# Layer 1's mixer in a two-layer fp32 trunk: a bank for the second spatial turn, spatial products at other steps, subtractions and square sums on VectorE

## The chip, the core and the metric

The kernel runs on one core of one Trainium2 chip, in one launch. The metric is the device time of an execution in microseconds: 994.84 as the median of 3 runs before the change. Of two kernels the faster is the one with the lower time; a difference counts from about 0.2%, 2 us.

TensorE multiplies, VectorE and ScalarE do elementwise work and can read PSUM, GpSimd does some elementwise work in SBUF and issues some DMAs, and SyncE's queue (SP) issues the loads of the weights.

## What is computed

An input x of 512 positions by 1024 features passes through two layers, each with a mixer and a gated feed-forward network (FFN) behind an RMS norm, and a final norm. Layer 1's mixer and the FFN are the parts that matter here:

```python
def chunked_spatial_gating(u, v, sgu_norm, w_spatial, b_spatial):
    b, s, _ = u.shape
    n = s // CHUNK                       # 4 chunks of 128 positions
    vn = rms_norm(v, sgu_norm).reshape(b, n, CHUNK, C_HEADS, C_HEAD_DIM)
    mask = jnp.tril(jnp.ones((CHUNK, CHUNK), dtype=w_spatial.dtype))
    ws = w_spatial * mask                # 8 heads, 128 x 128
    gate = jnp.einsum('hts,bnshc->bnthc', ws, vn) + b_spatial.T[None, None, :, :, None]
    return u * gate.reshape(b, s, C_WIDTH)

def gated_conv_ffn(x, w_gate, w_up, conv_w, conv_b, w_down):
    g = causal_dwconv3(jnp.einsum('bsd,df->bsf', x, w_gate), conv_w) + conv_b
    up = jnp.einsum('bsd,df->bsf', x, w_up)
    return jnp.einsum('bsf,fd->bsd', jax.nn.silu(g) * up, w_down)
```

In layer 1, u and v are the two halves of gelu(norm(h) @ w_in_odd), 1024 features each; the gated product goes through w_out_odd and is added to h.

## The kernel before

**Numbers.** Everything is float32. A factor is held as a high part, rounded to the type that TensorE multiplies fast (fp32r), and a low part, the remainder; a product is three matmuls, high by high, high by low and low by high (`mm3`, lines 132 to 135). A loaded block of weights (tag "raw", 4 buffers, issued on SP's queue) is split in one of two ways into tiles of 6 buffers each. `parts` (L127 to L129): ScalarE copies the high part, VectorE subtracts it for the low part. `summed` (L118 to L122): ScalarE writes the negated block as `lo` (L120), a DMA issued on GpSimd's queue adds the block to it (L121), ScalarE copies the high part (L122). A raw buffer is given to the next load when its readers are done, the accumulating DMA among them.

**PSUM.** Seven banks of 128x512 rotate among all products (`mm_bank`, L45); an eighth (`aux_bank`, L48) is shared by transposes and small sums. The instructions of one engine run in the order that a scheduler has fixed at build time; only semaphores order the engines against each other. A bank is given on when its last reader is done.

**Layer by layer.** h is kept feature by position, 8 tiles of 128x512. A projection loops over k, the 8 feature tiles, for four output banks. Each time a tile of h is complete, `Norm.add` writes its high and low part for the next stage (`hgh` on ScalarE, L175; `hgl` on VectorE, L176) and `Norm.square` adds its square to a running sum: the first square is written to the sum, the middle ones are squared on ScalarE (L188) and added on GpSimd (L189), the last is kept apart in some norms. The sums of squares over features are made with TensorE (`sst`, L197) and turned into 1/rms, which is applied after the projection.

**Layer 1's mixer** (`mixer1`) runs so: `u0`, the first half of u, over k; v, as a seven-product scheme with sums of blocks (`v_blocks`, L876; products in the order 1, 2, 6, 5, 7, 3, 4); `u1`, the second half of u, over k with four banks held throughout; then the output projection `oo` in two halves. The v scheme takes eight weight blocks as they are or summed; for products 7 and 4 it splits them with `summed`, for the others with `parts`. Between the products 2 and 6, `turn_spatial` (L1001) transposes the eight 128x128 spatial matrices in two groups of four (the tiles `wst`), each group into one bank, from which ScalarE takes the high and VectorE the low part (L1011, L1012). Both groups use the aux bank.

When v is complete, its norm's factor `rc_v` is worked out (square root on ScalarE, reciprocal and corrections on VectorE), and v is split into `vnh` (L1055) and `vnl` (L1056), eight tiles each, four per half of the heads. A spatial product (`spatial(j)`, one per head) is one `mm3` into a rotating bank `sp`, which VectorE multiplies by a gain into `gt` (L1072). `gated(j)` adds the bias and multiplies by u (L1079). `turned(j)` transposes `gt` into another bank `mT` (L1091) and splits it into `mx` (L1093, L1094), the moving factor of `oo`. These steps are set between the k-steps of `u1` and `oo` by a callback ahead of each k.

**The FFN.** Its gate and up projections use a seven-product scheme too (`both`, with sums of weight blocks `s12`, `s34` for gate and up; ScalarE and VectorE split them, L648 and L649); parts of products are kept (`kept`, L697, L707) while others run. The first pair of feature blocks of each layer is multiplied directly, before the norm's factor is applied to h; there the evacuation (`direct.evacuate`) multiplies by 1/rms: the gate's rows on VectorE (L571), then the convolution (L509), silu (ScalarE, L520), a multiply of the result by 1/rms on GpSimd (L574, two per layer), and the multiply of up by the result on VectorE (L577). The results are split again for the down projection (in layer 1 by `part`, L1149 to L1151).

Of the kernel before, what the change touches and what calls it, by code (L numbers as in the profile page):

```python
# [30 lines left out]
def tile_trunk(ctx: ExitStack, tc: tile.TileContext, x, norm_mix, norm_ffn, final_norm,  # L31
# [134 lines left out]
    class Norm:  # L166
# [13 lines left out]
        def square(self, k, order=lambda ins: ins):  # L180
            if self.n == 0:
                order(nc.scalar.activation(self.ssq, h[k], AF.Square))
            elif self.n == NK - 1 and self.apart:
                self.last = tp.tile([P, S], F32, tag="rstd", name=f"last_{self.name}")
                order(nc.scalar.activation(self.last, h[k], AF.Square))
            else:
                sq = tp.tile([P, S], F32, tag="sq", name=f"sq_{self.name}{k}")
                order(nc.scalar.activation(sq, h[k], AF.Square))  # L188
                nc.gpsimd.tensor_tensor(self.ssq, self.ssq, sq, ALU.add)  # L189
            self.n += 1  # L190

        def rstd_tokens(self):
# [296 lines left out]
    class Ffn:  # L489
# [58 lines left out]
        def direct(self, f, normed, sets, ch, before=lambda i, j: None):  # L548

            layer = self.layer  # L550
            banks = {}
            for js in sets:
                for i, k in enumerate(PAIRS):
                    for j in js:
                        before(i, j)
                        hi, lo = ch["gu"[j // 2], i // 4]
                        c = slice((j % 2) * P, (j % 2 + 1) * P)
                        if j not in banks:
                            banks[j] = mm_bank(f"gu{layer}_{f}_{j}")
                        mm3(banks[j], (hi[:, i % 4, c], lo[:, i % 4, c]), hg_k(k),  # L560
                            i == 0, i == NK - 1)

            def evacuate():
                r = self.r
                gates = []
                for j in range(2):
                    t = padded_tile()
                    if normed:
                        nc.scalar.copy(t[:, 2:], banks[j])
                    else:  # L570
                        nc.vector.tensor_tensor(t[:, 2:], banks[j], r, ALU.mult)  # L571
                    s = self.silu(self.conv(t, f + j), f + j)
                    if not normed:
                        nc.gpsimd.tensor_tensor(s, s, r, ALU.mult)  # L574
                    gates.append(s)
                for j, s in enumerate(gates):
                    nc.vector.tensor_tensor(s, banks[2 + j], s, ALU.mult)  # L577
                    self.act(f + j, s)

            return evacuate  # L580
# [65 lines left out]

        def halves(self, hi, lo, src):
            nc.scalar.activation(hi, src, AF.Copy)  # L648
            nc.vector.tensor_tensor(lo, src, hi.bitcast(F32), ALU.subtract)  # L649

        def both(self, f):

            layer, ap, n = self.layer, self.ap, f"{self.layer}_{f}"
            raws = ffn_weights(layer, f, [(key, half) for half in range(2) for key in "gu"])
            stat = {}

            def put(key, product, hi_lo, i):
                stat[key, product] = hi_lo[0][:, i], hi_lo[1][:, i]

            w = self.unit(f"a11_{n}")  # L660
            for i, key in enumerate("gu"):
                self.halves(w[0][:, i], w[1][:, i], raws[key, 0][0][:, :, :P])
                put(key, 1, w, i)
            for key in "gu":
                r0, r1 = raws[key, 0][0], raws[key, 1][0]
                s12, s34 = (wp.tile([P, 2, 4, P], F32, tag="sum", bufs=3, name=f"{x}{key}_{n}")
                            for x in ("s12", "s34"))
                nc.vector.tensor_tensor(s12[:, 0], r0[:, :, P:], r1[:, :, P:], ALU.add)
                nc.vector.tensor_tensor(s12[:, 1], s12[:, 0], r0[:, :, :P], ALU.subtract)  # L669
                w = self.unit(f"s12{key}_{n}")  # L670
                self.halves(*w, s12)
                put(key, 5, w, 0)
                put(key, 6, w, 1)
                nc.vector.tensor_tensor(s34[:, 0], r0[:, :, :P], r0[:, :, P:], ALU.subtract)
                nc.vector.tensor_tensor(s34[:, 1], r1[:, :, :P], s12[:, 1], ALU.subtract)
                hi, lo = (parts if f == NF - 2 else summed)(*raws[key, 1])
                for i, product in enumerate((2, 4)):
                    c = slice(i * P, (i + 1) * P)
                    stat[key, product] = hi[:, :, c], lo[:, :, c]
                w = self.unit(f"s34{key}_{n}")  # L680
                self.halves(*w, s34)
                put(key, 7, w, 0)
                put(key, 3, w, 1)

            banks = {"g": {}, "u": {}}
            kept = ap.tile([P, 3, HALF], F32, tag="kept", bufs=1, name=f"kept{n}")
            pads = [padded_tile() for _ in range(2)]
            lo, hi = slice(2, 2 + HALF), slice(2 + HALF, 2 + S)
            dst = {("g", 1): pads[0][:, lo], ("g", 6): pads[0][:, hi], ("g", 7): pads[1][:, hi],
                   ("g", 4): pads[1][:, lo]}  # L690
            dst.update({("u", product): kept[:, i, :] for i, product in enumerate((1, 6, 7))})
            onto = {2: 1, 5: 7, 3: 6}
            s, pending = {}, {}

            def after(key, product, ps):
                if (key, product) in dst:
                    nc.scalar.copy(dst[key, product], ps)  # L697
                elif product == 5 and (key, 7) not in pending:
                    pending[key, 5] = ps
                elif product in onto:  # L700
                    d = dst[key, onto[product]]
                    nc.vector.tensor_tensor(d, ps, d, ALU.add)  # L702
                if (key, product) == ("u", 4):
                    pending["u", 4] = ps
                if product == 7:
                    d = dst[key, 7]
                    nc.vector.tensor_tensor(d, pending[key, 5], d, ALU.add)  # L707

            for key, product in (("g", 1), ("u", 1), ("g", 5), ("g", 6), ("u", 5), ("u", 6),
                                 ("g", 2), ("g", 7), ("u", 2), ("u", 7), ("g", 4), ("g", 3),  # L710
                                 ("u", 4), ("u", 3)):
                after(key, product, self.multiply(banks[key], f"{key}{n}", product,
                                                  stat[key, product]))
                if (key, product) == ("g", 4):
                    s[1] = self.silu(self.conv(pads[1], f + 1), f + 1)
                elif (key, product) == ("g", 3):
                    s[0] = self.silu(self.conv(pads[0], f), f)
            nc.vector.tensor_tensor(s[1][:, HALF:], kept[:, 2, :], s[1][:, HALF:], ALU.mult)
            nc.vector.tensor_tensor(s[1][:, :HALF], pending["u", 4], s[1][:, :HALF], ALU.mult)
            self.act(f + 1, s[1])  # L720
            s0 = s[0].rearrange("p (a b) -> p a b", a=2)
            nc.vector.tensor_tensor(s0, kept[:, :2, :], s0, ALU.mult)
            self.act(f, s[0])
# [152 lines left out]
    def v_blocks(mp, w, v, v_gelu, loads, turn_spatial):  # L876
# [100 lines left out]
        turn_spatial()  # L977
        multiply(6, "a", keep(0, 1))
        for i in range(2):
            give(7, i, b12[i], True)  # L980
        multiply(5, "e", lambda i, ps: None)
        multiply(7, "a", c22)
        for i in range(2):
            give(3, i, last[i])
            give(4, i, b21[i], True)
        multiply(3, "e", c12)
        multiply(4, "a", lambda i, ps: v_gelu(2 + i, 0, ps))

    def mixer1(norm):
        w = w_in_odd[0]  # L990
        with tc.tile_pool(name="m1", bufs=1) as mp:
# [9 lines left out]
            def turn_spatial():  # L1001
# [1 line left out]
                wsT.append(wp.tile([P, NK, P], F32R, tag="sum", bufs=3, name="wsT_lo"))  # L1003
                wsT_hi, wsT_lo = wsT
                for q in range(2):
                    ps = aux_bank(f"wst{q}")
                    for i in range(4):
                        nc.tensor.transpose(ps[:, i * P : (i + 1) * P], ws[:, 4 * q + i, :], ident)
                    hi = wsT_hi[:, 4 * q : 4 * q + 4, :]
# [74 lines left out]
            def turned(j):  # L1084
# [9 lines left out]
                nc.vector.tensor_tensor(lo, ps, hi.bitcast(F32), ALU.subtract)  # L1094
                mix[j] = hi, lo

            def first_half(k):
                if 4 <= k < 6:
                    for j in range(4 * k - 16, 4 * k - 12):
                        spatial(j)  # L1100
                        if j < 4:
                            gated(j)
                elif k >= 6:
                    turned(2 * k - 12)
                    turned(2 * k - 11)

            in_group("u1", w, 512, False, u_done(1), 1, before=first_half)
            for j in range(4, 8):
# [1 line left out]

            def second_half(k):
                if 1 <= k < 4:
                    for j in ((4,), (5,), (6, 7))[k - 1]:
                        turned(j)

            nxt = Norm("f1", lambda k: prm1("ffn", k), apart=True)
# [4 lines left out]
    def ffn1(norm):  # L1121
        with tc.tile_pool(name="f1", bufs=1) as ap:
# [24 lines left out]
            def part(a, src, n):  # L1147
                hi = ap.tile([P, 2, HALF], F32R, tag="ahi", bufs=3, name=f"hi{n}_{a}")
                lo = ap.tile([P, 2, HALF], F32R, tag="alo", bufs=3, name=f"lo{n}_{a}")  # L1149
                nc.scalar.activation(hi, src, AF.Copy)  # L1150
                nc.vector.tensor_tensor(lo, src, hi.bitcast(F32), ALU.subtract)  # L1151
                return hi, lo

            def down(a):
# [181 lines left out]
```

## Time and profile before

| | us |
|---|---|
| runs before | 993.75, 994.84, 994.97 |
| the profiled execution | 995.75 |
| its span | 994.0 |
| TensorE busy | 976.8 |
| VectorE busy | 767.4 |
| ScalarE busy | 552.9 |
| GpSimd busy | 107.7 |
| mean granted TensorE clock | 0.995 |

All times in rows of the profile are counted from the start of the span of the one profiled execution. The run's time is 1.75 us more than its span, and 0.91 above the median. Layer 1's mixer lies between about 486 us and 630 us, its FFN behind it. A row of a timeline reads: start, length, engine, line, operation, tile written and tiles read, shapes, number of instructions in the row, and in brackets the engine's idle time before the row and what ended it.

### The profile page before, as it was taken

The page shows a single profiled execution, that of the slowest core. Times are in us where ns is not written, and L with a number is a line of the kernel's source. Part 1 is how long each engine was busy: PE and PEld are TensorE (multiplying, and loading weights), DVE is VectorE, ACT ScalarE, POOL GpSimd, SP SyncE. Part 2 cuts the span into 40 slices and gives each one's busy share as a digit, 9 for nine tenths or more (in the row PEclk, how much of TensorE's full clock was granted, in tenths as well). Part 3 has the DMA queues.
Part 4 walks back from the last instruction along what each step waited for, and adds up shares of the span by engine and source line. Part 5 has one row for each costly group of instructions (what it writes and reads, how often), then busy time and mean ns, then how long its engine had stood idle before and what let it go on. Part 6 is the DMA issues. An engine that isn't in the chain of part 4 may idle for free.

```text
span 994.0 us, 14507 instructions
## 1 busy us (share of the span) xinstructions
PE 976.8 (98%) x5619; PEld 859.3 (86%) x5619; DVE 767.4 (77%) x1151; ACT 552.9 (56%) x809; POOL 107.7 (11%) x123
## 2 busy tenths in 40 slices
PE   8999999999999999999998999999999999999997
PEld 6788888898999989999887878888998988989885
DVE  5877456968776687768996486479789989898996
ACT  5622346744653646535648854567566557565752
POOL 2132021200000000000221001203001001000000
PEclk9999999999999999999999999999999999999999
DMA  6522325454455544455315622345555656566432
GB/s 225 193 94 92 91 85 128 106 149 128 117 144 143 149 128 122 137 145 170 127 44 156 186 81 64 106 106 112 139 146 136 149 154 146 152 155 177 116 97 85
DMA packets 85361, 128.73 MB, mean 129 GB/s; under 512 B 4420, under 2 KB 53804, under 8 KB 85292
## 3 DMA queue, kind: packets, MB, share of 16 engines
q1 hardware_dynamic: 76172, 100.01, 32.3%
q0 software_dynamic: 7776, 26.22, 14.1%
q10 hardware_dynamic: 1344, 1.58, 0.5%
q8 instruction: 44, 0.72, 0.3%
q14 instruction: 25, 0.20, 0.1%
HBM read 99.47 MB, written 2.10 MB: 102 GB/s over the span
## 4 chain that ended last, share of the span: by engine, by line
PE 84%; DVE 7%; issue 4%; ACT 3%; DMA 1%; POOL 0%; SPq 0%; DVEq 0%; ACTq 0%; POOLq 0%
PE d L133 4%; PE d L134 4%; PE d L135 4%; PE gu L133 2%; PE gu L134 2%; PE gu L135 2%; PE g L133 1%; PE g L134 1%; PE oo L133 1%; PE oo L135 1%; PE oo L134 1%; PE oe L135 1%; PE oe L133 1%; PE g L135 1%; PE oe L134 1%
## 5 line engine op out<-in xcount | busy, mean ns | idle before, releaser
L509 DVE SCALAR_TENSOR_TENSOR c<-rows,prm,c 128x512 f32<-128x512 f32 x88 | 67.1, 778 | 2.8 <-ACT c L507 2.8
L134 PE MATMUL d<-a_lo,whi_d 128*128 128x512 f32 x176 | 68.6, 390 | 0.0
L135 PE MATMUL d<-a_hi,wlo_d 128*128 128x512 f32 x176 | 68.5, 389 | 0.0
L133 PE MATMUL d<-a_hi,whi_d 128*128 128x512 f32 x176 | 66.9, 390 | 0.0
L292 DVE TENSOR_TENSOR h<-d,h 128x512 f32<-128x512 f32 x48 | 32.5, 685 | 9.3 <-PE d L135 9.2
L134 PEld LDWEIGHTS d<-a_lo,whi_d 128*128 128x128 f32 x176 | 33.0, 188 | 7.3 <-DVE a_lo L249 0.2
L129 DVE TENSOR_TENSOR wlo_d<-raw_d,whi_d 128x1024 fp32r<-128x1024 f32 x22 | 26.8, 1220 | 16.1 <-ACT whi_d L128 16.1
L135 PEld LDWEIGHTS d<-a_hi,wlo_d 128*128 128x128 f32 x176 | 33.0, 188 | 6.8
L133 PEld LDWEIGHTS d<-a_hi,whi_d 128*128 128x128 f32 x176 | 32.8, 188 | 7.0
L520 ACT ACTIVATE s<-c,prm 128x512 f32<-128x512 f32 x44 | 31.2, 717 | 12.0 <-DVE c L509 11.9
L648 ACT ACTIVATE whi_s12u<-s12u 128x1024 fp32r<-128x1024 f32 x14 | 14.8, 1059 | 41.3 <-PE d L134 33.7
L121 POOL DMA_DIRECT2D wlo_g<-raw_g x17 | 14.8, 870 | 204.5 <-ACT wlo_g L120 172.3
L121 POOL DMA_DIRECT2D wlo_u<-raw_u x17 | 14.6, 861 | 199.7 <-ACT wlo_u L120 93.6
L175 ACT ACTIVATE hgh<-h,prm 128x512 fp32r<-128x512 f32 x24 | 17.3, 721 | 28.9 <-DVE h L292 28.9
L176 DVE SCALAR_TENSOR_TENSOR hgl<-h,prm,hgh 128x512 fp32r<-128x512 f32 x24 | 22.4, 940 | 13.3 <-ACT hgh L175 13.3
L507 ACT ACTIVATE c<-rows,prm 128x512 f32<-128x512 f32 x44 | 31.2, 717 | 1.6 <-DVE rows L702 1.0
L129 DVE TENSOR_TENSOR wlo_u<-raw_u,whi_u 128x1024 fp32r<-128x1024 f32 x17 | 21.2, 1250 | 13.8 <-ACT whi_u L128 13.8
L189 POOL TENSOR_TENSOR ssq_f<-ssq_f,sq_f 128x512 f32<-128x512 f32 x12 | 16.3, 1359 | 135.1 <-ACT sq_f L188 100.2
L648 ACT ACTIVATE whi_s12g<-s12g 128x1024 fp32r<-128x1024 f32 x14 | 14.8, 1060 | 28.8 <-DVE s12g L669 22.3
L128 ACT ACTIVATE whi_d<-raw_d 128x1024 fp32r<-128x1024 f32 x22 | 23.2, 1055 | 13.7 <-issue 2.6
L189 POOL TENSOR_TENSOR ssq_m<-ssq_m,sq_m 128x512 f32<-128x512 f32 x13 | 18.4, 1412 | 74.4 <-ACT sq_m L188 74.2
L128 ACT ACTIVATE whi_u<-raw_u 128x1024 fp32r<-128x1024 f32 x17 | 17.9, 1052 | 13.8 <-PE oe L134 4.4
(1419 smaller groups left out, 3670.0 us busy)
## 6 DMA issues: line engine op xcount, KB each, us to landing
raw_g<-in_w_ffn_gate_dram SPq DMA_DIRECT2D x36, 512.0 KB, 4.1
raw_u<-in_w_ffn_up_dram SPq DMA_DIRECT2D x36, 512.0 KB, 4.0
raw_d<-in_w_ffn_down_dram SPq DMA_DIRECT2D x22, 512.0 KB, 3.8
raw_dn<-in_w_ffn_down_dram SPq DMA_DIRECT2D x22, 512.0 KB, 4.3
wlo_g<-raw_g POOLq DMA_DIRECT2D x17, 512.0 KB, 4.5
wlo_u<-raw_u POOLq DMA_DIRECT2D x17, 512.0 KB, 4.6
raw_oe<-in_w_out_even_dram SPq DMA_DIRECT2D x8, 512.0 KB, 3.7
raw_g<-in_w_ffn_gate_dram SPq DMA_DIRECT2D x16, 256.0 KB, 3.1
```

The source lines that it names most:

```text
L121: nc.gpsimd.dma_start(lo, raw, accum_op=ALU.add)
L128: nc.scalar.activation(hi, raw, AF.Copy)
L129: nc.vector.tensor_tensor(lo, raw, hi.bitcast(F32), ALU.subtract)
L133: order(nc.tensor.matmul(ps, lhs[0], rhs[0], start=start, stop=False))
L134: nc.tensor.matmul(ps, lhs[0], rhs[1], start=False, stop=False)
L135: nc.tensor.matmul(ps, lhs[1], rhs[0], start=False, stop=stop)
L189: nc.gpsimd.tensor_tensor(self.ssq, self.ssq, sq, ALU.add)
L292: nc.vector.tensor_tensor(h[k], ps, h[k], ALU.add)
L507: nc.scalar.activation(c, t[:, 0:S], AF.Copy, scale=prm("cf", ft))
L509: self.convolved = nc.vector.scalar_tensor_tensor(c, t[:, i : S + i], prm("cf", i * NF + ft), c, op0=ALU.mult, op1=ALU.add)
L520: nc.scalar.activation(s, c, AF.Silu, bias=self.prm("bf", ft))
L648: nc.scalar.activation(hi, src, AF.Copy)
```

## The change

Six edits.

1. `Norm.square` adds the squares on VectorE, not on GpSimd (25 instructions in the program: 13 in mixer norms, 12 in FFN norms).
2. `direct.evacuate` multiplies by 1/rms on VectorE, not on GpSimd (4 instructions).
3. The v blocks of products 7 and 4, two each, are split by `parts`, not by `summed`: four ScalarE copies and four accumulating DMAs on GpSimd's queue go, four VectorE subtractions come.
4. The second group of spatial transposes takes one of the seven rotating banks. In the order of the program both groups stand one behind the other ahead of product 6; before, the second stood within product 5.
5. The spatial products, which stood four ahead of k=4 and four ahead of k=5 of `u1`, stand one at k=3, two each at 4, 5 and 6, and one at 7. The transposes of `gt` stood two at k=6, two at k=7 and four within `oo`; they stand one at 6, two at 7 and five within `oo`, the fourth with the fifth at its k=1.
6. In layer 1's FFN one low part (`lo` of `part(2, a11, 1)`, L1151) is issued behind the last low part of `both`'s sums.

```diff
@@ Norm.square
-                nc.gpsimd.tensor_tensor(self.ssq, self.ssq, sq, ALU.add)
+                nc.vector.tensor_tensor(self.ssq, self.ssq, sq, ALU.add)
@@ direct.evacuate
                     if not normed:
-                        nc.gpsimd.tensor_tensor(s, s, r, ALU.mult)
+                        nc.vector.tensor_tensor(s, s, r, ALU.mult)
@@ halves, both
             nc.scalar.activation(hi, src, AF.Copy)
-            nc.vector.tensor_tensor(lo, src, hi.bitcast(F32), ALU.subtract)
+            return nc.vector.tensor_tensor(lo, src, hi.bitcast(F32), ALU.subtract)
...
-                self.halves(*w, s34)
+                w_lo = self.halves(*w, s34)
                 put(key, 7, w, 0)
                 put(key, 3, w, 1)
+            self.last_low = w_lo
@@ v_blocks
         for i in range(2):
-            give(7, i, b12[i], True)
+            give(7, i, b12[i])
...
             give(3, i, last[i])
-            give(4, i, b21[i], True)
+            give(4, i, b21[i])
@@ turn_spatial
-                    ps = aux_bank(f"wst{q}")
+                    ps = aux_bank("wst0") if q == 0 else mm_bank("wst1")
@@ mixer1
+            SPATIAL = {3: (0,), 4: (1, 2), 5: (3, 4), 6: (5, 6), 7: (7,)}
+            TURNED = {6: (0,), 7: (1, 2)}
+
             def first_half(k):
-                if 4 <= k < 6:
-                    for j in range(4 * k - 16, 4 * k - 12):
-                        spatial(j)
-                        if j < 4:
-                            gated(j)
-                elif k >= 6:
-                    turned(2 * k - 12)
-                    turned(2 * k - 11)
+                for j in SPATIAL.get(k, ()):
+                    spatial(j)
+                    if j < 4:
+                        gated(j)
+                for j in TURNED.get(k, ()):
+                    turned(j)
...
-                    for j in ((4,), (5,), (6, 7))[k - 1]:
+                    for j in ((3, 4), (5,), (6, 7))[k - 1]:
                         turned(j)
@@ ffn1, part
                 nc.scalar.activation(hi, src, AF.Copy)
-                nc.vector.tensor_tensor(lo, src, hi.bitcast(F32), ALU.subtract)
+                with tc.issue_after(ffn.last_low.ins) if (a, n) == (2, 1) else ExitStack():
+                    nc.vector.tensor_tensor(lo, src, hi.bitcast(F32), ALU.subtract)
                 return hi, lo
```

## The prediction

> **What bounds the kernel now.** I read the page first, for how full TensorE is, then TensorE's timeline from end to end for every place where two matmuls stand further apart than their usual distance, and then, at each of those places, the chain of waits and the other engines' timelines.
>
> ```profile
> span 994.0 us, 14507 instructions
> PE 976.8 (98%) x5619; PEld 859.3 (86%) x5619; DVE 767.4 (77%) x1151; ACT 552.9 (56%) x809; POOL 107.7 (11%) x123
> ```
>
> TensorE is the bound: it is busy for all but 17.2 us of the span. The change takes no matmul away, so it can only gain where TensorE waits or is slowed, and lose where it makes TensorE wait anew. The rows below are TensorE's timeline at the places that the change touches: the last matmul before a stop, and the first after it with its idle time and releaser in brackets.
>
> ```profile
> 29.09 0.39 PE L135 MATMUL z<-hgh,wlo_z 128*128 128x512 f32 x1
> 29.89 0.38 PE L197 MATMUL sst_m<-small,ssq_m 128*128 128x1 f32 x2 [0.41 <-POOL ssq_m L189]
> ...
> 533.68 0.61 PE L933 MATMUL va<-whi_v,vs 128*128 128x512 f32 x2
> ...
> 539.58 0.39 PE L933 MATMUL ve<-wlo_v,vs 128*128 128x512 f32 x1
> 542.69 0.63 PE L1008 MATMUL wst<-ident,ws 128*128 128x128 f32 x4 [2.73 <-DVE wsT_lo L1012]
> ...
> 563.38 0.39 PE L133 MATMUL u<-whi_u,hgh 128*128 128x512 f32 x1
> ...
> 576.56 0.39 PE L134 MATMUL u<-wlo_u,hgh 128*128 128x512 f32 x1
> 578.78 0.50 PE L133 MATMUL sp<-vnh,wsT_hi 128*128 128x512 f32 x1 [1.83 <-DVE gt L1072]
> 579.12 0.40 PE L134 MATMUL sp<-vnl,wsT_hi 128*128 128x512 f32 x1
> ...
> 695.12 0.40 PE L639 MATMUL u_4e<-t,whi_s12u 128*128 128x256 f32 x2
> 696.16 0.39 PE L639 MATMUL u_4e<-t,wlo_s12u 128*128 128x256 f32 x1 [0.64 <-DVE wlo_s12u L649]
> 696.38 0.40 PE L639 MATMUL u_4e<-t,whi_s12u 128*128 128x256 f32 x2
> ...
> 697.33 0.28 PE L639 MATMUL u_4e<-t,wlo_s12u 128*128 128x256 f32 x1
> 697.89 0.50 PE L639 MATMUL u_4a<-t,whi_s12u 128*128 128x256 f32 x2 [0.28 <-ACT kept L697]
> 698.23 0.28 PE L639 MATMUL u_4a<-t,wlo_s12u 128*128 128x256 f32 x1
> ```
>
> Matmuls overlap, so I count from start to start. A 128x512 matmul takes 0.23 us so counted (twelve in 2.76, in the chain below), a 128x256 one 0.12 (696.16, two more, then the row two starts later: 0.22 for the late one and 0.12 each after).
>
> The chain of waits around the largest stop (start, length, what):
>
> ```profile
> 537.71 0.96 ACT wlo_v L120
> 538.67 0.95 ACT whi_v L122
> 539.62 0.95 ACT whi_v L128
> ...
> 540.60 1.24 DVE wlo_v L129
> ...
> 541.86 0.70 DVE wsT_lo L1012
> ...
> 542.69 0.63 PE wst L1008 x4
> 543.32 3.87 PE ve L933 x10
> 547.19 2.76 PE va L933 x12
> ```
>
> The second turn of the spatial weights can't start: it shares the one aux bank with the first turn, and VectorE empties that bank only after a low part that waits for three ScalarE passes, the first a negated copy for an accumulating DMA.
>
> **The change part by part.**
>
> *The bank and the four subtractions (edits 3 and 4).* The second turn gets a bank whose last reader, the gelu of u's first group, ran long before, and stands right behind the first turn, ahead of product 6. Neither turn waits then. From the last matmul ahead of the stop (539.58) to 542.69 are 3.11 us, 2.88 more than 0.23; and the ten `ve` matmuls behind it take 3.87 us where ten take 2.3, 1.6 more. Sum D: 4.5 us.
>
> It is gained only if product 7 doesn't inherit the wait. Without the stop it starts 4.5 us before 547.03, at 542.5. Its second high part on ScalarE is the 538.67 row; with two low copies of 0.96 ahead of it gone, it starts by 536.8 and ends by 537.8, and a subtraction of 1.24 on VectorE (idle there: the 540.60 pass had been waited for) ends by 539.0; product 7 reads that piece halfway, 2.76 later, at 545.3. Slack 6 us. Of products 3 and 4, one weight block is loaded again; what holds those loads is SP's queue:
>
> ```profile
> SPq L110 <- DMA wlo_v<-raw_v: 13.1, 2, 6.6
> ```
>
> (waiter, what ended the wait, total, times, longest.) SP stood 13.1 us, in two waits, for accumulating DMAs to finish reading a raw slot. With subtractions the slot is free when VectorE is done, so these loads start earlier, not later. ScalarE gets four passes fewer, VectorE four of 1.24 more, spread over some 12 us in which it is mostly idle. I take the whole 4.5; the lower bound is 0, the wait only moving to product 7.
>
> *The spread-out spatial products (edit 5).* E is the wait at 578.78: 2.22 from the row before, less 0.23, and 0.11 behind it: 2.1 us. Four products in a row need four banks beside the four of `u`, and three are left; the fourth waits for the first `gt`, and these rows (VectorE and ScalarE timelines) say why that is late:
>
> ```profile
> 561.02 1.06 ACT L128 ACTIVATE whi_u<-raw_u 128x1024 fp32r<-128x1024 f32 x1 [2.58 <-DMA raw_u<-in_w_in_odd_dram]
> ...
> 570.84 5.02 ACT L1055 ACTIVATE vnh<-v,rc_v 128x512 fp32r<-128x512 f32 x8 [0.84 <-DVE rc_v L237]
> ...
> 571.59 5.39 DVE L1056 SCALAR_TENSOR_TENSOR vnl<-v,rc_v,vnh 128x512 fp32r<-128x512 f32 x8 [0.79 <-ACT vnh L1055]
> ...
> 578.04 1.28 DVE L1072 TENSOR_TENSOR gt<-sp,g_bc 128x512 f32<-128x512 f32 x2
> ```
>
> The first `gt` starts 14.66 us after u's second group (563.38). After the change that group starts at 558.9 and lasts 12 x 0.23 = 2.73 per k. The first spatial product now stands at k=3, 558.9 + 3 x 2.73 = 567.1 for its high and 568.0 for its low operand; it needs four of the eight `vnh` and `vnl`. `vnh` starts 7.46 us after the group does (570.84 - 563.38). Of these, 2.58 are ScalarE waiting for a load of `u` (561.02), one of the loads that SP held back. If that goes, `vnh` starts at 558.9 + 4.88 = 563.8, four are done at 566.3 (0.63 each), four `vnl` at 567.2 (0.75 behind, 0.67 each): 0.8 us before each is wanted. The load has to be in by 553.9 (561.02 - 2.58 - 4.5). I place its issue at the last subtraction: 544.8 by my replay of the queues, 550.0 if the v block comes no earlier than before; with a landing time near 4.6, 549.4 to 554.6, so at worst 0.7 late, which the slack takes. The fourth product stands at k=5, 574.6, and its `gt` is done by 558.9 + 14.66 - 2.58 + 0.64 = 571.6. All 2.1 gained; bounds: 2.1, and 0.3 if the 7.46 stays (below).
>
> *Squares added on VectorE (edit 1), 25 instructions.* GpSimd's adds lengthen VectorE's own operations:
>
> ```profile
> 28.08 1.76 POOL L189 TENSOR_TENSOR ssq_m<-ssq_m,sq_m 128x512 f32<-128x512 f32 x1 [2.26 <-ACT sq_m L188]
> ...
> 492.76 1.37 POOL L189 TENSOR_TENSOR ssq_m<-ssq_m,sq_m 128x512 f32<-128x512 f32 x1 [0.87 <-ACT sq_m L188]
> 492.90 1.77 DVE L176 SCALAR_TENSOR_TENSOR hgl<-h,prm,hgh 128x512 fp32r<-128x512 f32 x1
> ...
> 496.06 0.75 DVE L176 SCALAR_TENSOR_TENSOR hgl<-h,prm,hgh 128x512 fp32r<-128x512 f32 x1 [0.79 <-ACT hgh L175]
> ```
>
> The same operation takes 1.77 beside a GpSimd add and 0.75 alone, 1.02 more. An add on VectorE costs about 0.60 from start to start (0.70 for the 128x512 row at 541.86, less the overlap). So where they overlapped VectorE gains 0.4 each, and where not it pays 0.6, which the stage must hold:
>
> ```profile
> 486.00:503.00 17.00, 17.00 (x76) 14.08 (x75) 15.27 (x16) 11.22 (x18) 10.11 (x7) 1.00 0.40 131
> 503.00:548.00 45.00, 42.27 (x188) 34.72 (x187) 34.42 (x54) 28.87 (x42) 4.79 (x4) 0.96 0.37 94
> ```
>
> (window: length, busy and count of PE, PEld, VectorE, ScalarE, GpSimd, granted clock, DMA share, GB/s.) In the first, the densest, seven adds cost 4.2 and give back about as much: five stretched operations there, some 4.4. Neutral. At the start of the kernel the wait A falls: GpSimd's add ran to 29.84; on VectorE it would end near 29.2, and TensorE comes at 29.32. A: 0.80 - 0.23 = 0.57; bounds 0 and 0.57.
>
> *The multiplies of the convolution (edit 2) and the low part moved back (edit 6).* F is two stops: 695.12 to 696.16, 1.04 less two matmuls, 0.80, with 0.10 behind it (0.22 - 0.12); and 697.33 to 697.89, 0.56 - 0.12 = 0.44, with 0.10 (0.34 - 0.24): 1.44 us. VectorE then ran
>
> ```profile
> 694.29 0.68 DVE L1151 TENSOR_TENSOR lo<-s,hi 128x512 fp32r<-128x512 f32 x1
> 694.89 1.22 DVE L649 TENSOR_TENSOR wlo_s12u<-s12u,whi_s12u 128x1024 fp32r<-128x1024 f32 x1
> ```
>
> The first now stands behind: 0.60 sooner. Two multiplies add 2 x 0.60 and free two stretched operations, 2 x 1.02. Net 1.44 sooner: `wlo_s12u` done at 694.67, wanted at 695.36. The copy that ends the second stop moves along. Bounds: +1.44, and -0.6 with no relief. A stop of 0.2 us in a later block, which the same queue shift may free, isn't counted.
>
> **Sum:** 0.57 + 4.5 + 2.1 + 1.44 = 8.6 us. The profiled run took 995.75, 1.75 above its span; that gives a span of 985.4 and a run of 987.1. It lay 0.91 above the median of 994.84; against that the same sum gives **986.2 us**.
>
> **A rule beside it.** The Trainium skill's page "TensorE: Matmul & The Clock Gate" (Part 1: The HAM clock gate) says that the clock halves after a whole idle window of about 3.4 us, not after a shorter stop. Here 2.73 us idle were enough for ten slow matmuls, while 1.83 us (578.78) were followed by matmuls at 0.23; by the rule neither stop slows anything and D would be 2.9, the sum 7.0 and the run 987.8. The rows decide.
>
> **The rivals.**
>
> *R1: the first spatial product meets a late `vn`.* If the 7.46 us stay, `vnh` starts at 566.4, four are done at 568.9, and TensorE waits 1.8 us at k=3. E gives 0.3: 986.2 + 1.8 = 988.0, or 989.7 if the clock drops as at 543. For it: statistics, square root table and `rc_v` are a serial chain; against it: 2.58 us of it is a load.
>
> *R2: only the bank counts.* D alone, all else even: 994.84 - 4.5 = 990.3.
>
> *R3: the change doesn't do what it says.* Product 7 or 3 waits for its pieces as the turn did, and D only moves: 994.84 - 4.1 = 990.7. Against it: the 6 us of slack.
>
> *R4: slower; VectorE gets no relief and takes over GpSimd's waits.* Two rows:
>
> ```profile
> 530.79 0.69 DVE L909 TENSOR_TENSOR vs<-vx,vs 128x512 fp32r<-128x512 f32 x1
> ...
> POOL s L574 <- ACT s L520: 8.3, 4, 2.6
> ```
>
> Seven adds put VectorE 4.2 us behind at 503, and it has next to no idle time up to the last row sum, whose low part (530.79) was done at 531.48 and is read by product 6 at 533.68; beyond 2.2 us every delay is TensorE's: 2.0, and at most 1.7 of slow clock. In layer 1's convolution VectorE waits in order for ScalarE's `s` as GpSimd did, half of 8.3, and adds 1.4: 5.5 us late at `wlo_s12u`, where there is no slack. 994.84 - (8.6 - 1.44) + 3.7 + 5.5 = 996.9. Against it: the stretched rows.
>
> **How the numbers follow.** The forecast has 0.56, R1 0.17, R2 0.11, R3 0.05, R4 0.06; 0.05 is left for a part of R4 that eats the gain. A measurement here tells 0.2%, 2 us, from nothing. So faster 0.89, same 0.05, slower 0.06. The range is 984.2 (nothing goes wrong, and 1.8 of run-to-run and unlisted waits fall) to 990.8, with R1 to R3 inside.
>
> **What would show it.** D: no idle time before the turns, `ve` at 0.23 throughout, granted clock 1.00 from 503 to 548. E: no `gt` named before `sp`; if a wait for `vnl` or `vnh` stands at the first product instead, R1. A: `sst_m` with no releaser. F: `u_4e` and `u_4a` without stops. Relief: `hgl` at 0.75 everywhere, and VectorE's busy time about even. The forecast is wrong if TensorE shows a wait of over 1 us anywhere between 486 and 600, or at product 6 above all.

## The result, and the profile after

| | before | after |
|---|---|---|
| median, 6 runs each, us | 994.9 (993.75 to 996.06) | 987.64 (986.8 to 988.39) |
| after / before | | 0.9926, interval 0.9913 to 0.9938 |
| profiled run: time, span, us | 995.75, 994.0 | 988.01, 986.2 |

The change saves 7.3 us where 8.6 were forecast. Lines of the changed kernel move by one to three in its rows (L933 is L934, L1008 is L1009, and so on). The page's first lines:

```profile
span 986.2 us, 14472 instructions
PE 973.6 (99%) x5619; PEld 857.2 (87%) x5619; DVE 776.0 (79%) x1184; ACT 549.5 (56%) x805; POOL 61.6 (6%) x90
```

TensorE is left with 12.6 us not busy, 4.6 less than before, and its busy time itself is 3.2 us lower, since slow matmuls count as busy for longer. VectorE took 33 more instructions: 25 adds and 4 multiplies near 0.69 and 4 subtractions of 1.22, some 25 us. Its busy time, which counts overlapping records once, rose by 8.6 us; record by record, the instructions that both kernels have take 9.5 us less. The reason shows in the durations: in the profile before, 20 VectorE instructions took over 0.1 us longer than the shortest of their kind, 15.2 us in all, and each ran beside a GpSimd operation; in the one after 5 do, 3.2 us in all, again each beside one. Fifteen of the 20 ran beside an add or a multiply that was moved, 12.1 us: 7.9 for the 25 adds, which cost VectorE 17.1, and 4.2 for the 4 multiplies, which cost 2.8. The groups show one kind, before and then after (mean ns of one behind the bar):

```profile
L176 DVE SCALAR_TENSOR_TENSOR hgl<-h,prm,hgh 128x512 fp32r<-128x512 f32 x24 | 22.4, 940 | 13.3 <-ACT hgh L175 13.3
```
```profile
L176 DVE SCALAR_TENSOR_TENSOR hgl<-h,prm,hgh 128x512 fp32r<-128x512 f32 x24 | 17.9, 750 | 11.8 <-ACT hgh L175 11.8
```

The places of the prediction, in the changed kernel's TensorE timeline (`u_4e`, `u_4a` and `u_4b` are banks of the up projection in the first `both` of layer 1's FFN):

```profile
28.44 0.39 PE L135 MATMUL z<-hgh,wlo_z 128*128 128x512 f32 x1
28.70 0.38 PE L197 MATMUL sst_m<-small,ssq_m 128*128 128x1 f32 x2
...
529.70 1.03 PE L1009 MATMUL wst<-ident,ws 128*128 128x128 f32 x8
...
533.08 0.62 PE L934 MATMUL va<-whi_v,vs 128*128 128x512 f32 x2
...
541.24 0.39 PE L934 MATMUL ve<-whi_v,vs 128*128 128x512 f32 x1
541.47 0.39 PE L934 MATMUL va<-whi_v,vs 128*128 128x512 f32 x1
...
557.79 0.39 PE L133 MATMUL u<-whi_u,hgh 128*128 128x512 f32 x1
...
565.95 0.39 PE L133 MATMUL sp<-vnh,wsT_hi 128*128 128x512 f32 x1
...
687.37 0.40 PE L639 MATMUL u_4e<-t,whi_s12u 128*128 128x256 f32 x2
687.61 0.28 PE L639 MATMUL u_4e<-t,wlo_s12u 128*128 128x256 f32 x1
...
694.24 0.39 PE L639 MATMUL u_4b<-hgh,wlo_u 128*128 128x256 f32 x1 [0.71 <-DMA wlo_u<-raw_u]
```

Both turns run as one row of eight without idle time, product 5 ends and product 7 starts at the usual 0.23, the first spatial product has no releaser, and `u_4e` reads its low part 0.24 behind its high part. A new stop stands at `u_4b`. The same by stages (columns as before):

```profile
486.00:503.00 17.00, 17.00 (x77) 14.08 (x76) 16.81 (x24) 10.84 (x16) 0.99 (x1) 1.00 0.34 110
503.00:548.00 45.00, 45.00 (x208) 37.48 (x207) 38.68 (x58) 29.02 (x44) 0.40 (x1) 1.00 0.23 82
```

TensorE fills the second window, with 208 matmuls counted where it had 188, at a granted clock of 1.00 where it had 0.96.

I sum TensorE's time beyond its usual distances, from start to start, for each profile below. The places are: the start of the kernel (to 33 us), the v stage (530 to 560), the spatial products (565 to 600), and the first `both` of layer 1's FFN (685 to 705).

| profile | start | v stage | spatial | `both` |
|---|---|---|---|---|
| before | 4.5 | 4.5 | 2.1 | 1.4 |
| after | 3.0 | 0 | 0 | 1.1 |

The four columns fall by 8.4 us and the span by 7.8. Most of the difference lies behind the last matmul, where the profile before has 7.3 us and the one after 7.7.

### The profile page after: what moved, and what is told of

Its sections match the earlier page's. It is cut to its first block, busy times and chain, and to the rows that moved or that the text cites. A ratio compares the mean times of both kernels' runs of the same rounds, so it can differ in the third digit from the quotient of the medians.

```text
span 986.2 us, 14472 instructions
## 1 busy us (share of the span) xinstructions
PE 973.6 (99%) x5619; PEld 857.2 (87%) x5619; DVE 776.0 (79%) x1184; ACT 549.5 (56%) x805; POOL 61.6 (6%) x90
## 4 chain that ended last, share of the span: by engine, by line
PE 93%; DMA 2%; DVE 2%; ACT 1%; issue 0%; SPq 0%; DVEq 0%; ACTq 0%; POOL 0%; POOLq 0%
PE d L134 4%; PE d L133 4%; PE d L135 4%; PE gu L133 2%; PE gu L135 2%; PE gu L134 2%; PE va L934 2%; PE u L133 1%; PE g L133 1%; PE oo L133 1%; PE g L134 1%; PE oo L135 1%; PE u L135 1%; PE oo L134 1%; PE g L135 1%; PE oe L134 1%
## 5 line engine op out<-in xcount | busy, mean ns | idle before, releaser
L509 DVE SCALAR_TENSOR_TENSOR c<-rows,prm,c 128x512 f32<-128x512 f32 x88 | 64.4, 747 | 2.8 <-ACT c L507 2.8
L520 ACT ACTIVATE s<-c,prm 128x512 f32<-128x512 f32 x44 | 31.3, 717 | 12.3 <-DVE c L509 12.1
L176 DVE SCALAR_TENSOR_TENSOR hgl<-h,prm,hgh 128x512 fp32r<-128x512 f32 x24 | 17.9, 750 | 11.8 <-ACT hgh L175 11.8
L133 PE MATMUL gu<-hgh,whi_u 128*128 128x512 f32 x64 | 25.4, 397 | 0.0
L133 PE MATMUL gu<-hgh,whi_g 128*128 128x512 f32 x64 | 25.4, 396 | 0.0
L133 PE MATMUL oo<-mx,whi_oo 128*128 128x512 f32 x64 | 25.2, 394 | 0.0
```

Source lines behind the costliest of these rows:

```text
L133: order(nc.tensor.matmul(ps, lhs[0], rhs[0], start=start, stop=False))
L509: self.convolved = nc.vector.scalar_tensor_tensor(c, t[:, i : S + i], prm("cf", i * NF + ft), c, op0=ALU.mult, op1=ALU.add)
L520: nc.scalar.activation(s, c, AF.Silu, bias=self.prm("bf", ft))
```

## The experiments

Each kernel was run for five rounds (4 to 12 runs) beside the kernel before; ratios are against that, and the changed kernel's own is 0.9926. Edits are numbered as above.

### One edit alone, or two

`bank`, the kernel before with edit 4:

```diff
-                    ps = aux_bank(f"wst{q}")
+                    ps = aux_bank("wst0") if q == 0 else mm_bank("wst1")
```

> The kernel before with edit 4 alone: the second turn of the spatial matrices in a rotating bank. My theory: the stop of 2.9 us in front of the second turn and the slow matmuls behind it go (4.5 us on TensorE at about 543), but ScalarE's and VectorE's chain from the accumulating DMAs over the held-back loads to vnh and gt isn't tied to TensorE and stays where it was (vnh at about 571, first gt at about 578), so TensorE waits at the spatial products for the 4.5 us that it is ahead: 994.9, no change, between 994 and 996, with over 5 us of idle time in front of sp. Rival (only the bank counts): 990.3.

995.34, ratio 1.0001 (0.9991 to 1.0011): no change, as forecast, and the rival falls. But the waits aren't where I put them: over 5 us were expected at the spatial products, and 1.02 stand there. TensorE's timeline, then ScalarE's:

```profile
545.19 0.50 PE L933 MATMUL va<-wlo_v,vs 128*128 128x512 f32 x1 [0.80 <-DMA wlo_v<-v]
...
552.58 0.50 PE L933 MATMUL ve<-whi_v,vs 128*128 128x512 f32 x1 [3.24 <-DVE v L941]
...
579.77 0.50 PE L133 MATMUL sp<-vnh,wsT_hi 128*128 128x512 f32 x1 [1.02 <-DVE gt L1072]
```
```profile
548.38 1.06 ACT L128 ACTIVATE whi_v<-v 128x1024 fp32r<-128x1024 f32 x1 [5.20 <-DMA v<-in_w_in_odd_dram]
549.35 1.04 ACT L120 ACTIVATE wlo_v<-raw_v 128x1024 fp32r<-128x1024 f32 x1
550.29 1.04 ACT L122 ACTIVATE whi_v<-raw_v 128x1024 fp32r<-128x1024 f32 x1
551.24 0.56 ACT L955 COPY v<-va 128x512 f32<-128x512 f32 x1
```

The reloaded v block arrives late; ScalarE waits 5.20 us for it and has three splits in line ahead of the copy (L955) that VectorE needs to free the bank of product 3. So most of the stop moves to product 3 (3.24, and slow matmuls behind it again), a part to product 7's own low part, and 1.02 stays at the spatial products.

`subs`, the kernel before with edit 3:

```diff
-            give(7, i, b12[i], True)
+            give(7, i, b12[i])
...
-            give(4, i, b21[i], True)
+            give(4, i, b21[i])
```

> The kernel before with edit 3 alone: the four blocks of products 7 and 4 split by a subtraction on VectorE. Both turns still share the aux bank; in the built order the second turn now stands 16 matmuls into product 6, and VectorE empties the bank only behind two of the new subtractions. My theory: the stop isn't gone but stands in product 6 and is 4 to 5 us long, with slow matmuls behind it, so D gives nothing; the loads are no longer held back, so the wait of 2.1 us at the spatial products goes: 992 to 994. Rival (the subtractions alone cure the stop): 988 to 990.

993.27, 0.9977 (0.9967 to 0.9987), inside the range. The spatial wait is gone; the stop stands where it was expected, with slow matmuls behind it, but 3.1 us of idle time long where 4 to 5 were expected:

```profile
537.21 1.11 PE L1008 MATMUL wst<-ident,ws 128*128 128x128 f32 x4 [3.10 <-DVE wsT_lo L1012]
```

`bank_subs`, both of these:

> The kernel before with edits 3 and 4 together. My theory: the 4.5 us of the stop and, without any spreading, also the 2.1 us at the spatial products, since the first gt comes about 3 us earlier against u's second group: 988.3, between 987.5 and 989.3. Rival (the wait at the spatial products needs edit 5): 990.4.

988.0, 0.9926 (0.9912 to 0.994). Nothing is left in the v stage and at the spatial products, with the spatial products still four and four. Two edits worth 0 and 2.3 us alone are worth 7 together.

`subs_squares`, the kernel before with edits 3 and 1 (the line of `Norm.square`):

> The kernel before with edits 3 and 1: the four subtractions and the square sums on VectorE, the turns still sharing the aux bank. The subtractions alone moved the stop into product 6 (3.3 us and slow matmuls). My theory: without GpSimd's adds VectorE's list is about 2 us earlier in this stage and the second turn stands 24 and not 16 matmuls into product 6, so the bank is free in time and the new bank of edit 4 isn't needed: 988.0, between 987.3 and 989, no idle time in front of wst. Rival (the stop stays, somewhat shorter): 990 to 992.

987.28, 0.9922 (0.9909 to 0.9934), at the lower edge of its range, with no stop at the second turn. So the bank has a substitute: squares added on VectorE. They put VectorE's list further ahead of TensorE: the low part of the last row sum, which was done 2.2 us before product 6 read it, is done 4.3 us before in the changed kernel (528.74 by the row below, against the row at 533.08 above); about 0.4 of that is the second turn, which now stands ahead of product 6. All 14 profiles agree: this low part ends 0.8 to 0.9 us behind the start of the first turn in the six with the adds on GpSimd, and 1.0 us ahead of it in the eight with the adds on VectorE. The other half is the built order: the second turn stands 24 matmuls into product 6 here and 16 in `subs`, 1.8 us later. Together these are some 3.5 us, little more than the stop of `subs`.

```profile
528.06 0.68 DVE L910 TENSOR_TENSOR vs<-vx,vs 128x512 fp32r<-128x512 f32 x1
```

`spread`, the kernel before with edit 5:

> The kernel before with edit 5 alone. My theory: the first product, now at k=3, meets a vn that isn't ready, 1.8 us of waiting there in place of 2.1 at the fourth: 994.6, between 993.8 and 996. Rival (spreading cures the wait by itself): 992.8.

995.26, 0.9997 (0.9988 to 1.0007): no change. In its one profile the wait at the first product is 0.24 us idle for `vnh`, not 1.8, and the wait of 2.1 is gone; a gain of up to 1.2 us would still lie in the interval, the rival's 2.1 doesn't. ScalarE's wait for the load of `u` happens to be 1.08 us in this profile, where it was 2.58, so it doesn't tell what the spreading does.

### One edit undone in the changed kernel

`no_bank` (edit 4 undone):

> The changed kernel without edit 4: both turns share the aux bank. In the built order the second turn stands at the end of product 6's first 24 matmuls, and VectorE empties the bank behind two subtractions. My theory: a stop of 1.5 to 3 us there, with or without slow matmuls behind it: 989.1 to 992.2. Rival (the subtractions alone cure the stop): 987.6, as the changed kernel.

987.78, 0.9922 (0.9907 to 0.9937): a miss. The rival is right here: no stop at the second turn.

```profile
535.55 0.39 PE L934 MATMUL va<-wlo_v,vs 128*128 128x512 f32 x1
535.78 0.29 PE L1009 MATMUL wst<-ident,ws 128*128 128x128 f32 x1
```

I had left out that edit 1 brings VectorE forward; `subs_squares` shows that edits 1 and 3 are enough. They are only just enough: VectorE empties the bank at 535.69, 0.09 us before the turn starts. In the time, edit 4 is superfluous beside edits 1 and 3, and edit 1 beside 3 and 4.

`no_spread` (edit 5 undone):

> The changed kernel without edit 5: four spatial products ahead of k=4 and four ahead of k=5. My theory: the wait of 2.1 us at the fourth product was the late gt, and that is early now, so spreading is worth next to nothing: 987.6 to 988.2, a wait of under 0.5 us in front of sp. Rival (edit 5 is what cures the wait): 989.7, with 2 us idle in front of sp.

988.47, 0.9937 (0.9921 to 0.9953), 0.3 above the range, with no wait at any spatial product: spreading isn't what cured it.

`no_squares` (edit 1 undone):

> The changed kernel without edit 1: the squares added on GpSimd. My theory: the 0.57 us wait for ssq_m at the start comes back, the two waits at about 21 us in the changed kernel's profile come from a load that arrived late for a start that was early, so they aren't owed to the squares; VectorE's operations beside GpSimd's adds are long again but hidden: 988.2. Rival (the adds on VectorE made the waits at 21 us): 987.0.

987.83, 0.994 (0.9916 to 0.9963): the same within noise, with two runs at 993. The wait for `ssq_m` didn't come back, but another stands just ahead of it, and it is GpSimd's doing: its add stretches an `hgl` to 1.78 us, where one alone takes 0.75, and TensorE loses 1.0 us start to start.

```profile
26.66 1.33 POOL L189 TENSOR_TENSOR ssq_m<-ssq_m,sq_m 128x512 f32<-128x512 f32 x1 [2.05 <-ACT sq_m L188]
```
```profile
26.75 1.78 DVE L371 SCALAR_TENSOR_TENSOR hgl<-h,prmmix,hgh 128x512 fp32r<-128x512 f32 x1
```
```profile
28.59 0.50 PE L134 MATMUL z<-hgl,whi_z 128*128 128x512 f32 x1 [0.77 <-DVE hgl L371]
```

Of the waits at 21 us, which the changed kernel has too, 0.3 us stand in this profile, so they don't need the adds on VectorE.

`p7_dma` and `p4_dma` (edit 3 undone for product 7, or for product 4):

```diff
-            give(7, i, b12[i])
+            give(7, i, b12[i], True)
```
```diff
-            give(4, i, b21[i])
+            give(4, i, b21[i], True)
```

> The changed kernel with product 7's two blocks split by the accumulating DMA again, product 4's by subtraction. My theory: the DMA reads the raw slot until it lands, about 7 us after its issue, so one v block is loaded again late, ScalarE waits for it in order ahead of the copy that frees product 3's bank, and TensorE waits ahead of product 3 (ve, released by VectorE's add to v) as in the run with edit 4 alone, less what VectorE is earlier now: 2 to 5 us more than the changed kernel, 989.5 to 992.5. Rival (what counts is the aux bank and VectorE's work, not the loads): 987.6.

> The changed kernel with product 4's two blocks split by the accumulating DMA again, product 7's by subtraction. My theory: these DMAs hold slots for loads of u that are wanted late, so it costs little: 987.6 to 988.6. Rival (all four DMAs count alike): as much as product 7's, 989.5 or more.

`p7_dma`: 990.91, 0.9953 (0.9941 to 0.9964), with the same releaser ahead of product 3 as in `bank`:

```profile
547.93 0.50 PE L934 MATMUL ve<-whi_v,vs 128*128 128x512 f32 x1 [1.40 <-DVE v L942]
...
551.50 0.50 PE L934 MATMUL ve<-whi_v,vs 128*128 128x512 f32 x1 [0.55 <-DVE v L942]
```

`p4_dma`: 989.37, 0.9937 (0.9924 to 0.9951), 0.8 over its range. The v stage and the spatial products have no wait in it; its profile has a stop of 2.5 us at `u_4b` instead, the one that the next experiments are about, with slow matmuls behind it. So product 7's DMAs are what counts in the v stage; in `p7_dma` SP stands 6.9 us for one of them to be done with its slot.

### The new stop at `u_4b`

`no_scale` (edit 2 undone):

> The changed kernel without edit 2: the convolution's multiply by 1/rms on GpSimd. My theory: the new wait of 1 us for the accumulating DMA of wlo_u (its landing took 6.6 us against 4.6 before, beside two loads that were issued within 1.3 us of it) goes, because the loads are issued apart again; part of the stops at u_4e and u_4a comes back, as the low part of s12u is only 0.6 us earlier than in the kernel before: between 987.0 and 988.4, same within noise. Rival (edit 2 is what cures u_4e): 1.4 us of stops there, 988.1 or more, with no wait at u_4b.

987.88, 0.9924 (0.9911 to 0.9938). The stop at `u_4b` is gone, and the two at `u_4e` and `u_4a` are back in full, 1.43 us with what stands behind them: edit 6 without edit 2 cures nothing.

```profile
687.98 0.38 PE L639 MATMUL u_4e<-t,wlo_s12u 128*128 128x256 f32 x1 [0.52 <-DVE wlo_s12u L649]
...
689.82 0.39 PE L639 MATMUL u_4a<-t,whi_s12u 128*128 128x256 f32 x1 [0.39 <-ACT kept L698]
```

The DMA issues tell why edit 2 made the new stop. First the changed kernel (GpSimd's and SP's queues), then `no_scale`:

```profile
681.70 0.86 POOL L121 DMA_DIRECT2D wlo_g<-raw_g  x1 [12.56 <-ACT wlo_g L120]
687.62 0.86 POOL L121 DMA_DIRECT2D wlo_u<-raw_u  x1 [5.06 <-ACT wlo_u L120]
...
686.33 0.35 SPq L110 DMA_DIRECT2D raw_dn<-in_w_ffn_down_dram  x1
686.76 0.39 SPq L110 DMA_DIRECT2D raw_g<-in_w_ffn_gate_dram  x1
```
```profile
677.03 0.86 POOL L121 DMA_DIRECT2D wlo_g<-raw_g  x1
688.86 0.86 POOL L121 DMA_DIRECT2D wlo_u<-raw_u  x1 [10.97 <-ACT wlo_u L120]
...
685.60 0.38 SPq L110 DMA_DIRECT2D raw_g<-in_w_ffn_gate_dram  x1
```

With the multiply on VectorE, the scheduler puts ScalarE's negated copy of the gate's block behind a later silu; its DMA goes out at 681.70, not 677.03, and `raw_dn`, which waits for its slot, goes out right ahead of `raw_g` and of the DMA that `u_4b` needs. That one then lands 6.6 us after its issue, 4.5 in `no_scale`. Across profiles its landing goes with its distance from the load issued ahead of it (issue times and the landing line of each profile):

| profile | issued after `raw_g`, us | to landing, us |
|---|---|---|
| before | 3.26 | 4.6 |
| `no_scale` | 3.26 | 4.5 |
| after | 0.86 | 6.6 |
| `no_squares` | 0.86 | 6.5 |
| `p7_dma` | 0.82 | 6.6 |
| `no_spread` | 0.61 | 7.0 |
| `p4_dma` | 0.05 | 8.4 |
| `no_bank` | -0.07 | 8.5 |

The stop goes with it, from 0.6 to 2.7 us idle; that the distance sets the landing is read from these rows and wasn't tested by itself. In `no_bank` and `p4_dma` slow matmuls follow the stop, and this place costs 4.4 and 4.2 us, against 1.1 in the changed kernel. The profiled run of `no_bank` is its slowest, 991.73, and most of what it has over the changed kernel's profiled run, 3.7 us, lies here. The scatter of some kernels with edit 2 (`no_bank` 986.76 to 991.73; `no_scale`, without it, 987.58 to 988.02) would fit; but `bank`, also without it, scatters from 994.15 to 998.02.

`u4_sub`, the changed kernel with this block split on VectorE:

```diff
-                hi, lo = (parts if f == NF - 2 else summed)(*raws[key, 1])
+                hi, lo = (parts if f == NF - 2 or (layer, f, key) == (1, 4, "u")
+                          else summed)(*raws[key, 1])
```

> The changed kernel with one more block, u's second of feature blocks 4 and 5 in layer 1's FFN, split by a subtraction on VectorE and not by the accumulating DMA. My theory: the wait for that DMA at u_4b (0.9 us in the changed kernel's profile, up to 2.8 in others with edits 2 and 6) goes and VectorE, idle for 1.6 us there, hides the subtraction: 986.6, with no stop at u_4e, u_4a or u_4b. Rival (VectorE passes the subtraction on): a new wait for wlo_s34u, 987.6 or more.

986.27 (985.62 to 986.91), 0.9908 (0.9895 to 0.9921): the stop is gone and no other took its place.

```profile
692.56 0.28 PE L639 MATMUL u_4b<-hgh,whi_u 128*128 128x256 f32 x1
692.68 0.28 PE L639 MATMUL u_4b<-hgl,whi_u 128*128 128x256 f32 x1
692.80 0.28 PE L639 MATMUL u_4b<-hgh,wlo_u 128*128 128x256 f32 x1
```

It has the lowest time of all kernels here, 1.4 us under the changed kernel; the two weren't run side by side, and the intervals of their ratios overlap.

## Why the prediction was right or wrong

**The sign and the size.** 987.64 lies in the range, 1.4 above the forecast of 986.2. The sum was 8.6 and 7.3 came. (The lower end of the range, by its own working, is 986.2 - 1.8 = 984.4, not 984.2.) Two rivals' times lie nearer, R1's 988.0 and the clock rule's 987.8, but by luck: `vn` isn't late (E below), and the slow matmuls of D did go.

**D (4.5 us): right, with an incomplete cause.** The stop and the slow matmuls are gone to the last tenth, and product 7 inherits nothing. The prediction worked out both halves, bank and subtractions, and the runs show that it takes both, or the subtractions with edit 1. R2, the bank alone at 990.3, is refuted by `bank`: alone it is worth nothing. R3, the stop only moving, is what each half does by itself.

**E (2.1 us): right in mechanism, not owed to edit 5.** The distance from u's second group to `vnh` was to fall from 7.46 to 4.88; it is 562.59 - 557.79 = 4.80:

```profile
562.59 5.02 ACT L1056 ACTIVATE vnh<-v,rc_v 128x512 fp32r<-128x512 f32 x8 [0.84 <-DVE rc_v L237]
```

So four of `vnh` are done by 565.1, 0.85 before the first product. R1 falls. The distance goes with ScalarE's wait for the load of `u`: 7.46 with 2.58 before, 6.61 with 1.74 in `bank`, 5.95 with 1.08 in `spread`, 4.99 with 0.1 in `p4_dma`, and 4.8 with none in the others. But the same holds with the products four and four (`bank_subs`, `no_spread`): the loads that came in time were the cure, and the spreading, to which the prediction gave the 2.1, added nothing that can be measured.

**A (0.57 us): right in mechanism, the gain isn't shown in the time.** `sst_m` no longer waits (28.70 above). All six profiles with the adds on GpSimd have a wait between 27 and 30 us: 0.57 for `ssq_m` in four (before, `bank`, `subs`, `spread`), 1.0 for a stretched `hgl` in two (`bank_subs`, `no_squares`). The eight with the adds on VectorE have neither. In exchange 1.2 us of short waits stand at 21 us in the changed kernel's profile, which the prediction didn't have; such waits are 0 to 1.4 us in the eight, 0 to 0.3 in the six, and what sets them stays open. What TensorE loses at the start differs by up to 2.4 us between the profiles (4.5 before, 2.1 in `no_spread`), at a wait for x to arrive and slow matmuls behind it among others, and `no_squares` is within noise of the changed kernel, so half a microsecond can't be seen in the time. On average the six lose 1.1 us more at the start than the eight; the slow matmuls ahead of 11 us, in four of the six and one of the eight, are part of that.

**F (1.44 us): the step that failed.** The prediction said that VectorE's list would be 1.44 sooner and both stops go; they went. It followed VectorE and didn't carry ScalarE's order and the DMAs behind it on to the next product: 1.07 us came back at `u_4b`. Net 0.4, and a loss of about 3 in the profiles of `no_bank` and `p4_dma`, where the issues fall closer together and the clock drops behind the stop.

**Relief on VectorE: right in kind, too large in size.** `hgl` costs 750 ns throughout and the kernel is faster, so R4 falls. But the busy time was to stay about even, and it rose by 8.6 us: the multiplies give back more than they cost, the adds less than half.

Together: 4.5 from D, 2.1 from E and 0.4 from F are 7.0, beside the 7.3 measured; the 1.5 that the two profiles show at the start isn't counted, since the start differs by over 1 us between profiles with the same adds there.

**The clock rule.** The prediction set the Trainium skill's rule (page "TensorE: Matmul & The Clock Gate", Part 1: The HAM clock gate), which needs an idle window of about 3.4 us, against ten slow matmuls after 2.73 us idle. More stops are to be seen now. The six longest, all shorter than the page's window, were each followed by a stretch at a granted clock of 0.50:

| profile | idle, us | clock 0.50 |
|---|---|---|
| `p4_dma` | 2.53 | 695.5 to 698.6 |
| `no_bank` | 2.68 | 698.2 to 701.5 |
| before | 2.73 | 543.3 to 546.5 |
| `spread` | 2.90 | 542.6 to 545.9 |
| `subs` | 3.10 | 537.2 to 542.8 |
| `bank` | 3.24 | 553.9 to 557.1 |

The stretch need not begin at once. In `no_bank` TensorE runs on at the full clock for 1.5 us behind the stop, and only then drops (stages with columns as before):

```profile
696.63 0.39 PE L639 MATMUL u_4b<-hgh,wlo_u 128*128 128x256 f32 x1 [2.68 <-DMA wlo_u<-raw_u]
```
```profile
696.60:698.20 1.60, 1.57 (x13) 1.58 (x14) 0.08 (x1) 0.00 (x0) 0.00 (x0) 0.97 0.15 24
698.20:701.50 3.30, 3.30 (x17) 3.30 (x17) 0.34 (x1) 0.37 (x1) 0.00 (x0) 0.50 0.98 330
```

Apart from the first 11 us of the kernel, no stop up to the 1.83 us of the kernel before was followed by one. In these runs a loss was seen from 2.53 us on.

## What to carry to other kernels

An accumulating DMA that makes a low part also holds its source buffer until it lands, here some 7 us; ask which load is waiting for that buffer and which in-order engine then stands in front of the load. When a stop on the bounding engine has two causes, taking away one shows nothing: pair the edits before judging either. When a list of one engine is brought forward, carry the new order on to the DMAs that the next stage needs.

## What the runs showed of the hardware

A 512 KB accumulating DMA landed 4.5 us after its issue when the last load had been issued 3.3 us before, and 8.4 us after when it had been issued 0.05 us before, with one more load just ahead. TensorE's granted clock fell to 0.50 for 3 to 6 us behind each of six stops of 2.53 to 3.24 us, once 1.5 us after the stop had ended. Moving 29 adds and multiplies from GpSimd to VectorE made 15 other VectorE operations 12.1 us shorter in all, up to 1.1 us each, against the 19.9 us that the moved ones take there.
